# Attention scores of two heads on 64 array rows each, and an earlier fetch of cached keys and adaLN weights, in a two-layer hybrid decoder step

## The chip, the cores and the metric

The kernel runs on one core of a Trainium2 chip. The metric is the time of one execution on the device in microseconds (us), lower is better. Before the change three runs took 1097.65, 1100.09 and 1101.35 us; the median is 1100.09 us.

## The reference

One inference step of two decoder layers for a prompt of 512 tokens and eight sample rows that share all weights (width 1024, float32). Each layer is: adaLN-modulated RMSNorm, one input projection, two mixers, each times a SiLU gate, one output projection, adaLN gate, residual. Layer 0 has a short convolution and a windowed attention of 16 heads with 64 features; layer 1 has multi-scale pooling and retention. The change touches the attention of the prompt and the fetch of the cached keys for the sample rows. For the prompt it comes to this:

```python
q, k, v = (a.reshape(Bn, L, H_B, HD_B) for a in (q, k, v))      # 16 heads of 64
qf = q.astype(jnp.float32) * (Dh ** -0.5)
# scores q k^T plus ALiBi over three windows (128,1), (512,4), (2048,16),
# merged by their softmax denominators: one softmax with a bias that holds log(count)
y_b = o.reshape(Bn, L, W_B) * jax.nn.silu(gb)
```

The sample rows attend to 256 of 1024 cached keys and values in the same three patterns. k and v of all tokens are outputs too.

## The kernel before

Features lie on the partitions, tokens on the columns (512 of the prompt and 8 of the sample group). To reach float32 accuracy with the faster matmul type, each factor x is split into a high part (ACT copies x to the type fp32r) and a low part (VectorE, DVE, subtracts the high part from x); a product is then high × high, high × low and low × high.

A weight tile of 128 output features is computed by `product` (line 315): eight steps (k = 0 to 7), each with six matmuls of 256 or 264 columns (`mm3`, line 295). After each step `advance` (line 304) issues a part of the conversion of later weights: the high part on ACT at k = 1 (`w_hi`), low parts on DVE (`w_lo`), the load of a raw tile on SP (`w_raw`, four buffers). Then comes `tick` (line 198), the clock of the issue order. Small work is put into its queues: `at(n, ...)` runs n steps later; `put(..., after=n)` at the first step from n on, one per step; `put_fill` at a step in which no `put` was due; `put2` at even steps. The order of issue is thus written out by hand, and each engine, and SP's queue of DMA issues too, executes its instructions in that order.

Layer 0 begins with the attention, `head_pair(p)` (line 457), eight times. A pair has two heads (e = 0, 1) of 64 features, so that one weight tile is v, k, gate or q of both heads. The tiles come in the order v, k, gate, q, 32 steps in all; the scores and all that follows them run beside the tiles of the next pair. Times after the q tile are counted from its end, with Q0 = 5 as base for scores, turns and weighings.

- The plain k (`kf`, line 585) is copied by ACT out of PSUM. `k_dup` (line 473) then makes for each head a tile with that head's 64 rows of k twice, on partitions 0 to 63 and 64 to 127, with four DMAs from SBUF to SBUF. `k_split` (line 481), 7 and 9 steps after the k tile, makes high and low parts of each doubled tile.
- q (lines 600 to 612): for each head one tile with the high part of its 64 rows on its own half of the partitions and the low part on the other half (`q_lo`).
- `score(e, qb)` (line 508), four blocks of 128 queries for each head: two matmuls over all 128 rows, first with the high, then with the low part of the doubled k, with N = 256, 256, 384, 512 columns. DVE adds the bias and takes the minimum of the negated scores (line 521), ACT takes Exp one step later, `norm` (line 529) divides three steps later: DVE's reciprocal, then DVE (even blocks) or ACT (odd blocks) scales.
- `turn(e, g)` (line 539) transposes the probabilities on TensorE in three groups and splits them; `weigh(e, jb)` (line 547) multiplies them with v. Scores, turns, weighings, the turned v (`v_out`), the rows of q and the adaLN products share four PSUM buffers (`aux`).
- `q_rows` (line 487) turns q of the sample rows and writes it to DRAM. Four steps later `window_load` (line 495) loads it back, broadcast to all partitions, then the cached keys (three DMAs, 1 MB) and a tile of layer 1's adaLN weights (1 MB); both of these use the pool `big` with three buffers. DVE multiplies keys by q and sums (`window_scores`, `window_sums`, lines 568 and 572) 5 and 8 steps later; the adaLN product (`ada`, line 360) follows 8 steps later.

The order of the attention of one pair at the end of the q tile is written as:

```python
for e, fn, ticks in (
    (0, score, (0, 1, 3, 4)), (1, score, (6, 7, 9, 10)), (0, turn, (11, 13, 15)), (0, weigh, (18, 19, 21, 23)),
    (1, turn, (17, 20, 22)), (1, weigh, (25, 26, 27, 28)),
):
```

All DMAs go through SP's queue (`load`, line 156). After the attention come the convolution tiles of layer 0, the output projection and layer 1, which the change leaves alone.

Of the kernel before, what the change touches and what calls it, by code (L numbers as in the profile page):

```python
# [29 lines left out]

# columns of the packed constants
C_ID = 0
# [54 lines left out]
def hybrid_kernel(ctx: ExitStack, tc: tile.TileContext, a, o):  # L87
# [21 lines left out]
    def tr(n=T):  # L109
        return tt(n, F32R)  # L110
# [68 lines left out]

# [1 line left out]
    now, seqn = [0], [0]  # L181
# [34 lines left out]

# [1 line left out]
    csm = cp.tile([P, C_W], F32, name="csm")  # L218
# [21 lines left out]

# [1 line left out]
    w_in = [a["w_in_e"], a["w_in_o"]]  # L242
# [61 lines left out]
    def advance(k):  # L304
        # weights of the tiles that come next, a part at each step of this tile
        if k == 1 or (k == 5 and n_split[0] < cur[0] + 2):
            w_hi()
        if k in (3, 6):
            w_lo((0,))
        if k in (4, 7):  # L310
            w_lo((1,))
        if k in (5, 7) and n_raw[0] < n_split[0] + 4:
            w_raw()
# [15 lines left out]

# [1 line left out]
    def ada_load(layer, kind, j):  # L331
# [35 lines left out]

# [1 line left out]
    def h_hi(layer, j, xp, xs):  # L369
# [12 lines left out]

# [1 line left out]
    warm = cp.tile([P, 1], F32, name="warm")  # L384
# [62 lines left out]
    load(csm[:, P:C_W], a["c_small"][:, P:C_W])  # L447
# [1 line left out]
    yB, yA = [None] * KT, [None] * KT  # L449
# [7 lines left out]
    def head_pair(p):  # L457
# [14 lines left out]

        def k_dup(kf):
            st["kd"] = []
            for e in range(2):
                kd = tt(S)
                for h in range(2):
                    load(kd[64 * h:64 * h + 64], kf[64 * e:64 * e + 64])
                st["kd"].append(kd)

        def k_split(e):
            kh, kl = tr(S), tr(S)
            act(kh, st["kd"][e])
            at(2, lo_of, kl, st["kd"][e], kh)
            st["k", e] = (kh, kl)

        def q_rows():
            pq = aux([NB, P])
            nc.tensor.transpose(pq, zs[0][:, 32 + p, :], ident)
            qt = tt(P, p=NB)  # L490
            act(qt, pq)
            at(1, load, qdr[p], qt)
            at(4, window_load)

        def window_load():
            st["qb"] = t4().rearrange("p (b d) -> p b d", b=NB)
            load(st["qb"], qdr[p].partition_broadcast(P))
            kw = big().rearrange("p (t b d) -> p t b d", t=2, b=NB)
            c = a["cache_win_k"][0].rearrange("b s h d -> s b (h d)")[:, :, p * P:(p + 1) * P]
            load(kw[:, 0], c[896:1024])  # L500
            load(kw[0:96, 1], c[512:896].rearrange("(n s) b d -> n s b d", s=4)[:, 0])
            load(kw[96:128, 1], c[0:512].rearrange("(n s) b d -> n s b d", s=16)[:, 0])
            for t in range(2):
                at(5 + 3 * t, put2, window_scores, t, kw)
            raw = ada_load(1, "ss", p)
            at(8, ada, 1, "ss", p, raw)

        def score(e, qb):
            if qb == 0:
                st["bt"] = bt[e]  # L510
                st["mn", e], st["ls", e] = mk(cp, [P, 4], F32, "mn", 4), mk(cp, [P, 4], F32, "ls", 4)
                st["E", e] = []
            n, N = (qb + 1) * P, max(H0, (qb + 1) * P)
            kh, kl = st["k", e]
            mn, ls = st["mn", e][:, qb:qb + 1], st["ls", e][:, qb:qb + 1]
            s = aux([P, S])
            qs = st["q", e][:, qb * P:(qb + 1) * P]
            mm(s[:, 0:N], qs, kh[:, 0:N], True, False)
            mm(s[:, 0:N], qs, kl[:, 0:N], False, True)
            sb = tt(n)  # L520
            nc.vector.tensor_tensor_reduce(  # L521
                out=sb, in0=s[:, 0:n], in1=bt[e][:, S - n:S], scale=1.0, scalar=3e38, op0=ALU.add, op1=ALU.min,
                accum_out=mn,
            )
            st["E", e].append(sb)
            at(1, act, sb, sb, ACTF.Exp, mn, -1.0, ls)
            at(3, norm, e, qb)
# [49 lines left out]

        # v, k, q and gate tiles, each followed by what depends on it
        vps = ps01[0] if p == 0 else z_tile(0, 48 + p, h0)
# [7 lines left out]
        sample_z(0, 40 + p, kps)  # L587
        at(0, k_dup, kf)
        at(1, load, o["k_t"][p], kf)
        at(7, k_split, 0)  # L590
        at(9, k_split, 1)
        gps = z_tile(0, 56 + p, h0)
# [5 lines left out]
        for e in range(2):  # L598
            load(bt[e], a["c_bias"][2 * p + e])
        qps = z_tile(0, 32 + p, h0)  # L600
        for e in range(2):
            r = slice(64 * e, 64 * e + 64)
            st["q", e] = tr(S)
            act(p2(st["q", e][r]), qps[r, :, 0:H0], ACTF.Copy, scale=-0.125)

        def q_lo():
            for e in range(2):
                r, r_ = slice(64 * e, 64 * e + 64), slice(64 - 64 * e, 128 - 64 * e)
                stt(p2(st["q", e][r_]), qps[r, :, 0:H0], -0.125, p2(f(st["q", e][r])), ALU.mult, ALU.subtract)
            sample_z(0, 32 + p, qps)  # L610

        at(1, q_lo)
        for e, fn, ticks in (
            (0, score, (0, 1, 3, 4)), (1, score, (6, 7, 9, 10)), (0, turn, (11, 13, 15)), (0, weigh, (18, 19, 21, 23)),
            (1, turn, (17, 20, 22)), (1, weigh, (25, 26, 27, 28)),
        ):
            for i, n in enumerate(ticks):
                put(fn, e, i, after=Q0 + n)
        put_fill(q_rows, after=8)

# [6 lines left out]

# [1 line left out]
    uc = mk(cp, [P, KT, 15 + NB], F32, "uc", 1)[:, :, 0:2 + 2 * NB]  # L629
# [9 lines left out]
    def soft_scores():  # L639
        # softmax over window rows and the new row, (batch, head) on partitions  # L640
        prod = tt(P).rearrange("p (b k e) -> p b k e", b=NB, k=KT)
# [46 lines left out]
    def window_weigh(b0):  # L688
        # two batches at a time: rows (batch, half of the heads, head), columns (head in the half, feature)
        pd = aux([P, 512])  # L690
# [106 lines left out]

# [1 line left out]
    def out_tile(layer, m, ps, halves=(0, 1)):  # L799
# [15 lines left out]
    def scaled(j, out=None):  # L815
        # input of layer 1 without its norm's factor and without the shift
        x = xT[j] if out is None else out
        vtt(x[:, S:T], xT[j][:, S:T], mA[1][:, j, 0:NB], ALU.mult)
        act(x[:, 0:S], xT[j][:, 0:S], ACTF.Copy, scale=mA[1][:, j, 8:9])
        xT[j] = x  # L820
# [39 lines left out]

    # the first tiles of layer 1 take x without the norm's factor, which is put to their products
    h1, r1 = [[tr(), tr()] for _ in range(KT)], tt()
# [35 lines left out]

# [1 line left out]
    G = [1.0 - 2.0 ** (-5.0 - h) for h in range(H_D)]  # L900
# [6 lines left out]
    def ret_head(h):  # L907
# [97 lines left out]

        # sample group: state update and read, all batches of this head
        def v_rows():
# [64 lines left out]

        # tiles
        st["vh"] = t4(dt=F32R).rearrange("p (a i d) -> p a i d", a=4, i=2)
# [64 lines left out]

# [1 line left out]
    spl = t4()[:, 0:KT * NB * 15].rearrange("p (k b w) -> p k b w", k=KT, b=NB)  # L1141
# [76 lines left out]

# [1 line left out]
    xo = [[tt(512) for _ in range(2)] for _ in range(4)]  # L1220
# [14 lines left out]
    def rows(m, blocks):  # L1235
        # rows of tokens: their squares and their product with the gain
        hf, c = m // 4, (m % 4) * P
# [37 lines left out]

    # the last tile: one half of the tokens after the other
    m = KT - 1
# [25 lines left out]
def layout(i):  # L1303
    # the arrays in the order in which the tiles are read
    def tiles(w):
# [33 lines left out]
def results(r):  # L1339
    # features back to the last axis  # L1340
    conv = r["conv_t"].transpose(2, 1, 0).reshape(2 + 2 * NB, D)
# [29 lines left out]
```

## Time and profile before

| | us |
|---|---|
| median of three runs | 1100.09 |
| lowest, highest run | 1097.65, 1101.35 |
| profiled execution, first to last instruction (its span) | 1099.1 |
| TensorE matmuls (PE) busy | 1046.0 (95%) |
| VectorE (DVE) busy | 652.6 (59%) |
| ScalarE (ACT) busy | 501.5 (46%) |
| mean granted TensorE clock | 0.985 |

The profile is one execution on the chip; the page gives its span alone as its time, 1.0 us below the median of the runs. PE is the matmul part of TensorE and PEld its weight loads, which overlap with matmuls; SPq is SP's queue, which issues the DMAs. Busy time counts overlapping instructions once. An idle time is shown in square brackets with what ended it. The attention stage of the eight pairs lies at about 50 to 350 us. Engines work in parallel, so a busy engine need not be what sets the time.

### The profile page before, as it was taken

To read this page: it belongs to the slowest core of one execution; us is meant where nothing else is said; L and a number is where in the kernel's file an instruction comes from. 1 tells how busy PE (TensorE), PEld (TensorE's weight loads), DVE (VectorE), ACT (ScalarE), POOL (GpSimd) and SP (SyncE) were. 2 spreads that over 40 slices of the span, in tenths; PEclk is the share of its full clock that TensorE was granted. 3 is DMA by queue.
4 is the path that set the end of the run, shared out by engine and by line. 5 is a ranking of instruction groups with operands and counts; after the bars stand their busy time and mean duration, and the time that the engine had idled before them with its cause. 6 is when DMAs were issued, how large, how long until landed. Compare 5 with 4: busy or idle time off the path is not lost.

```text
span 1099.1 us, 21017 instructions
## 1 busy us (share of the span) xinstructions
PE 1046.0 (95%) x8592; PEld 1000.6 (91%) x8592; DVE 652.6 (59%) x1484; ACT 501.5 (46%) x906; POOL 27.4 (2%) x45
## 2 busy tenths in 40 slices
PE   3999899989989999999999989999999999999996
PEld 1698898889989899999999989999999999999996
DVE  6557676767668544446444487555746667664443
ACT  4575568556755322223243364545444444332333
POOL 3000000000000000000000040000000000000000
PEclk9899999999999999999999999999999999999998
DMA  8365654565446463542653326372543532225212
GB/s 350 149 218 182 201 179 147 166 213 184 140 158 192 154 205 125 192 157 83 205 204 130 120 69 235 112 249 87 206 164 117 195 124 87 87 87 184 97 68 78
DMA packets 84736, 173.15 MB, mean 158 GB/s; under 512 B 7720, under 2 KB 47752, under 8 KB 81560
## 3 DMA queue, kind: packets, MB, share of 16 engines
q1 hardware_dynamic: 84640, 171.81, 46.7%
q8 instruction: 67, 1.10, 0.4%
q14 instruction: 29, 0.24, 0.1%
HBM read 149.40 MB, written 18.65 MB: 153 GB/s over the span
## 4 chain that ended last, share of the span: by engine, by line
PE 77%; DMA 8%; DVE 6%; ACT 5%; issue 2%; SPq 1%; DVEq 0%; ACTq 0%
PE mm L160 64%; PE aux L160 11%; ACT t L140 4%; DMA t<-t 4%; DMA big<-in_cache_win_k 3%; DVE t L146 2%; DVE wlo L146 1%; SPq L157 1%; DVE t L521 1%; DMA wraw<-in_w_in_e 1%; DMA v<-vdr 1%; ACT whi L140 1%; DMA out_k_t<-t 1%; ACT L140 0%; PE aux L1242 0%
## 5 line engine op out<-in xcount | busy, mean ns | idle before, releaser
L160 PE MATMUL mm<-t,whi 128*128 128x256 f32 (+1 forms) x4608 | 766.0, 288 | 7.7 <-ACT t L140 5.6
L160 PEld LDWEIGHTS mm<-t,whi 128*128 128x128 f32 x4608 | 644.3, 190 | 31.6 <-issue 17.2
L160 PE MATMUL mm<-t,wlo 128*128 128x256 f32 (+2 forms) x2304 | 468.2, 284 | 0.0
L160 PEld LDWEIGHTS mm<-t,wlo 128*128 128x128 f32 x2304 | 361.2, 190 | 0.0
L146 DVE TENSOR_TENSOR wlo<-wraw,whi 128x512 fp32r<-128x512 f32 x288 | 194.3, 701 | 51.8 <-ACT whi L140 51.3
L140 ACT ACTIVATE whi<-wraw 128x1024 fp32r<-128x1024 f32 x144 | 151.8, 1054 | 96.9 <-PE mm L160 61.1
L140 ACT ACTIVATE t<-t 128x520 fp32r<-128x520 f32 (+3 forms) x124 | 75.8, 616 | 214.8 <-DVE t L149 98.3
L146 DVE TENSOR_TENSOR t<-t,t 128x520 fp32r<-128x520 f32 (+6 forms) x172 | 112.4, 654 | 96.4 <-ACT t L140 95.0
L140 ACT ACTIVATE t<-mm 128x512 f32<-128x512 f32 (+3 forms) x124 | 61.0, 512 | 126.6 <-PE mm L160 125.9
L140 ACT ACTIVATE t<-aux 128x512 fp32r<-128x512 f32 (+7 forms) x148 | 66.5, 465 | 57.7 <-PE aux L160 20.4
L146 DVE TENSOR_TENSOR t<-aux,t 128x512 fp32r<-128x512 f32 (+6 forms) x120 | 61.7, 514 | 24.0 <-ACT t L140 17.5
L160 PE MATMUL aux<-t,v 128*128 128x512 f32 (+2 forms) x224 | 52.3, 338 | 18.5 <-DVE t L146 18.5
L160 PE MATMUL aux<-t,t 128*128 128x256 f32 (+2 forms) x320 | 63.2, 311 | 0.0
L160 PEld LDWEIGHTS aux<-t,v 128*128 128x128 f32 x224 | 36.1, 197 | 21.5 <-DVE t L146 20.4
L143 DVE COPY zs<-mm 128x8 f32<-128x8 f32 x76 | 12.2, 161 | 60.6 <-ACT t L140 60.5
L160 PEld LDWEIGHTS aux<-t,t 128*128 128x128 f32 x320 | 47.0, 188 | 0.7
L140 ACT ACT_TABLE_LOAD x32 | 41.1, 1283 | 8.1 <-DVE mn L521 3.5
L140 ACT ACTIVATE t<-t,mn 128x128 f32<-128x128 f32 (+1 forms) x64 | 35.3, 551 | 12.9 <-DVE mn L521 12.8
L521 DVE CUSTOM_DVE_ANT_0 t<-aux,t 128x128 f32<-128x128 f32 (+1 forms) x64 | 30.7, 488 | 9.6 <-PE aux L160 9.4
L149 DVE SCALAR_TENSOR_TENSOR big<-v,ksc,big 128x256 f32<-128x256 f32 x64 | 27.7, 481 | 10.1 <-ACT big L140 9.7
L146 DVE TENSOR_TENSOR t<-mm,t 128x512 f32<-128x512 f32 (+1 forms) x24 | 16.6, 690 | 26.7 <-PE mm L160 17.4
L160 PE MATMUL aux<-big,scT 128*32 128x256 f32 x384 | 27.4, 406 | 0.3 <-DMA big<-in_ada_e 0.3
(145 smaller groups left out, 591.6 us busy)
## 6 DMA issues: line engine op xcount, KB each, us to landing
wraw<-in_w_in_e SPq DMA_DIRECT2D x64, 512.0 KB
wraw<-in_w_in_o SPq DMA_DIRECT2D x48, 512.0 KB
big<-in_ada_e SPq DMA_DIRECT2D x12, 1024.0 KB
big<-in_ada_o SPq DMA_DIRECT2D x12, 1024.0 KB
wraw<-in_w_out_e SPq DMA_DIRECT2D x16, 512.0 KB
big<-in_state_ret SPq DMA_DIRECT2D x16, 512.0 KB
out_new_ret_sample<-big SPq DMA_DIRECT2D x16, 512.0 KB
wraw<-in_w_out_o SPq DMA_DIRECT2D x16, 512.0 KB
```

What stands on the lines that cost most here:

```text
L140: return nc.scalar.activation(out=out, in_=in_, func=func, scale=scale, **kw)
L143: return nc.vector.tensor_copy(out, in_)
L146: return nc.vector.tensor_tensor(out=out, in0=in0, in1=in1, op=op)
L149: return nc.vector.scalar_tensor_tensor(out=out, in0=in0, scalar=scalar, in1=in1, op0=op0, op1=op1)
L157: return nc.sync.dma_start(out=out, in_=in_)
L160: nc.tensor.matmul(out, lhsT=lhsT, rhs=rhs, start=start, stop=stop)
L521: nc.vector.tensor_tensor_reduce(out=sb, in0=s[:, 0:n], in1=bt[e][:, S - n:S], scale=1.0, scalar=3e38, op0=ALU.add, op1=ALU.min, accum_out=mn,
```

## The change

- k is not copied any more: `k_dup` is gone, and `k_split` makes one high and one low tile of the plain k, 3 steps after the k tile. q too has one high and one low tile with both heads, each head on its own 64 partitions.
- A score call does both heads for one block of queries. It takes two PSUM buffers and issues three products (high × high, high × low, low × high), alternating between head 0 (partitions 0 to 63) and head 1 (64 to 127): six matmuls over 64 rows. What follows a score (`soft`) is as before, for one head and then the other.
- The scores run at steps 0, 2, 3, 5 after the base, the turns of both heads interleaved at 11 to 17, the weighings of head 0 at 18 to 21 and those of head 1 at 22 to 26.
- The cached keys and the adaLN weights are loaded by `window_load` 5 steps after the gate tile, that is in the q tile. The broadcast of q is a function of its own, `q_load`, four steps after `q_rows`, which may run from step 4 instead of 8. The key products come 7 and 10 steps after `q_load`, the adaLN product 20 steps after its load.

The rest of the diff removes comments. Its core:

```diff
-        def k_dup(kf):
-            st["kd"] = []
-            for e in range(2):
-                kd = tt(S)
-                for h in range(2):
-                    load(kd[64 * h:64 * h + 64], kf[64 * e:64 * e + 64])
-                st["kd"].append(kd)
-
-        def k_split(e):
+        def k_split(kf):
             kh, kl = tr(S), tr(S)
-            act(kh, st["kd"][e])
-            at(2, lo_of, kl, st["kd"][e], kh)
-            st["k", e] = (kh, kl)
+            act(kh, kf)
+            at(2, lo_of, kl, kf, kh)
+            st["k"] = (kh, kl)
...
-            at(4, window_load)
+            at(4, q_load)
 
         def window_load():
-            st["qb"] = t4().rearrange("p (b d) -> p b d", b=NB)
-            load(st["qb"], qdr[p].partition_broadcast(P))
             kw = big().rearrange("p (t b d) -> p t b d", t=2, b=NB)
...
+            st["kw"] = kw
+            raw = ada_load(1, "ss", p)
+            at(20, ada, 1, "ss", p, raw)
+
+        def q_load():
+            st["qb"] = t4().rearrange("p (b d) -> p b d", b=NB)
+            load(st["qb"], qdr[p].partition_broadcast(P))
             for t in range(2):
-                at(5 + 3 * t, put2, window_scores, t, kw)
-            raw = ada_load(1, "ss", p)
-            at(8, ada, 1, "ss", p, raw)
+                at(7 + 3 * t, put2, window_scores, t, st["kw"])
 
-        def score(e, qb):
+        def score(qb):
+            N = max(H0, (qb + 1) * P)
+            ss_ = [aux([P, S]) for _ in range(2)]
+            for c, (x, y) in enumerate(((0, 0), (0, 1), (1, 0))):
+                for e in range(2):
+                    r = slice(64 * e, 64 * e + 64)
+                    mm(ss_[e][:, 0:N], st["q"][x][r, qb * P:(qb + 1) * P], st["k"][y][r, 0:N], c == 0, c == 2)
+            for e in range(2):
+                soft(e, qb, ss_[e])
+
+        def soft(e, qb, s):
...
-            s = aux([P, S])
-            qs = st["q", e][:, qb * P:(qb + 1) * P]
-            mm(s[:, 0:N], qs, kh[:, 0:N], True, False)
-            mm(s[:, 0:N], qs, kl[:, 0:N], False, True)
...
-        at(0, k_dup, kf)
         at(1, load, o["k_t"][p], kf)
-        at(7, k_split, 0)
-        at(9, k_split, 1)
+        at(3, k_split, kf)
...
+        at(5, window_load)
         qps = z_tile(0, 32 + p, h0)
...
+        qh, ql = tr(S), tr(S)
+        st["q"] = (qh, ql)
+        act(p2(qh), qps[:, :, 0:H0], ACTF.Copy, scale=-0.125)
 
         def q_lo():
...
+            stt(p2(ql), qps[:, :, 0:H0], -0.125, p2(f(qh)), ALU.mult, ALU.subtract)
             sample_z(0, 32 + p, qps)
 
         at(1, q_lo)
+        for qb, n in enumerate((0, 2, 3, 5)):
+            put(score, qb, after=Q0 + n)
         for e, fn, ticks in (
-            (0, score, (0, 1, 3, 4)), (1, score, (6, 7, 9, 10)), (0, turn, (11, 13, 15)), (0, weigh, (18, 19, 21, 23)),
-            (1, turn, (17, 20, 22)), (1, weigh, (25, 26, 27, 28)),
+            (0, turn, (11, 13, 15)), (1, turn, (12, 14, 17)), (0, weigh, (18, 19, 20, 21)), (1, weigh, (22, 23, 24, 26)),
         ):
             for i, n in enumerate(ticks):
                 put(fn, e, i, after=Q0 + n)
-        put_fill(q_rows, after=8)
+        put_fill(q_rows, after=4)
```

## Rows read from the trace of the kernel before

**Rows 1.** The profile's page, busy time of the engines over the whole span.
```profile
PE 1046.0 (95%) x8592; PEld 1000.6 (91%) x8592; DVE 652.6 (59%) x1484; ACT 501.5 (46%) x906; POOL 27.4 (2%) x45
```

**Rows 2.** Windows, two head pairs: stretch, length, busy PE, PEld, DVE, ACT, POOL, PEclk, DMA, GB/s.
```profile
101.35:139.38 38.03, 34.48 (x272) 32.97 (x271) 25.32 (x62) 23.09 (x46) 0.00 (x0) 0.96 0.55 169
139.38:173.83 34.45, 32.82 (x272) 31.51 (x271) 25.32 (x62) 23.11 (x46) 0.00 (x0) 1.00 0.56 181
```

**Rows 3.** Waits of PE, 60 to 350 us: us in total, times, longest.
```profile
PE aux L160 <- DVE t L146: 18.5, 8, 3.5
```

**Rows 4.** Timeline of PE at three of these waits: start, us, instruction, idle before it.
```profile
96.72 0.50 PE L160 MATMUL aux<-t,v 128*128 128x512 f32 x1 [2.15 <-DVE t L146]
...
133.19 0.61 PE L160 MATMUL aux<-t,v 128*128 128x512 f32 x1 [3.55 <-DVE t L146]
...
204.47 0.50 PE L160 MATMUL aux<-t,v 128*128 128x512 f32 x1 [2.46 <-DVE t L146]
```

**Rows 5.** Windows, two equal stretches: behind the wait at 133.19, and later.
```profile
133.44:136.85 3.41, 3.41 (x15) 3.20 (x15) 2.69 (x5) 1.52 (x4) 0.00 (x0) 0.50 0.10 25
...
137.00:140.41 3.41, 3.41 (x31) 3.41 (x30) 1.80 (x4) 3.03 (x5) 0.00 (x0) 1.00 0.31 123
```

**Rows 6.** The chain of waits, 101 to 140 us: start, us, what.
```profile
120.65 8.38 DMA t<-t
...
129.11 0.63 ACT t L140
...
132.58 0.57 DVE t L146
```

**Rows 7.** Waits of ACT, 60 to 330 us.
```profile
ACT t L140 <- DMA t<-t: 47.7, 7, 8.0
...
ACT whi L140 <- DMA wraw<-in_w_in_e: 1.2, 1, 1.2
```

**Rows 8.** Timeline of SP's queue, 110 to 124 us: DMA issues.
```profile
112.73 4.21 SPq L157 DMA_DIRECT2D big<-in_cache_win_k  x3
116.99 1.69 SPq L157 DMA_DIRECT2D big<-in_ada_o  x1
...
119.29 3.46 SPq L157 DMA_DIRECT2D t<-t  x4
```

**Rows 9.** Windows, the stretch in which these transfers land; the last two columns are DMA.
```profile
118.50:130.50 12.00, 11.15 (x97) 10.03 (x95) 7.57 (x9) 2.98 (x6) 0.00 (x0) 1.00 1.03 310
```

**Rows 10.** Timeline of PE, 141 to 145.8 us: score matmuls (aux) and what follows each.
```profile
141.40 0.40 PE L160 MATMUL aux<-t,t 128*128 128x256 f32 x2
141.63 0.64 PE L160 MATMUL mm<-t,whi 128*128 128x256 f32 x4
...
145.08 0.63 PE L160 MATMUL aux<-t,t 128*128 128x512 f32 x2
145.55 0.52 PE L160 MATMUL mm<-t,whi 128*128 128x256 f32 x3
```

**Rows 11.** Timeline of PE, 126.6 to 129.6 us: an adaLN product between projection matmuls.
```profile
127.33 0.39 PE L160 MATMUL mm<-t,wlo 128*128 128x256 f32 x2
127.65 1.07 PE L160 MATMUL aux<-big,scT 128*32 128x256 f32 x16
128.65 0.75 PE L160 MATMUL mm<-t,whi 128*128 128x256 f32 x4
129.24 0.40 PE L160 MATMUL mm<-t,wlo 128*128 128x256 f32 x2
```

**Rows 12.** The page's groups, weight loads (all aux products of two tiles): busy, mean ns.
```profile
L160 PEld LDWEIGHTS aux<-t,t 128*128 128x128 f32 x320 | 47.0, 188 | 0.7
```

**Rows 13.** Windows, from a pair's first Exp to its last scaling.
```profile
105.58:118.64 13.06, 13.06 (x107) 12.87 (x107) 8.48 (x32) 11.69 (x29) 0.00 (x0) 1.00 0.50 151
```

**Rows 14.** Timeline of DVE, 121 to 129 us: key product and its sum.
```profile
122.03 1.23 DVE L146 TENSOR_TENSOR big<-big,v 128x1024 f32<-128x1024 f32 x1 [1.83 <-DMA big<-in_cache_win_k]
...
124.38 1.21 DVE L573 TENSOR_REDUCE t<-big 128x16 f32<-128x1024 f32 x1
```

More of the change, by code (lines that the diff above doesn't have):

```diff
@@ L502, in window_load @@
             load(kw[96:128, 1], c[0:512].rearrange("(n s) b d -> n s b d", s=16)[:, 0])
-            for t in range(2):
-                at(5 + 3 * t, put2, window_scores, t, kw)
-            raw = ada_load(1, "ss", p)
-            at(8, ada, 1, "ss", p, raw)
-        def score(e, qb):
+            st["kw"] = kw
[4 more added lines that the diff above has]
+            load(st["qb"], qdr[p].partition_broadcast(P))
+            for t in range(2):
+                at(7 + 3 * t, put2, window_scores, t, st["kw"])
[9 more added lines that the diff above has]
+        def soft(e, qb, s):
             if qb == 0:
-                st["bt"] = bt[e]
                 st["mn", e], st["ls", e] = mk(cp, [P, 4], F32, "mn", 4), mk(cp, [P, 4], F32, "ls", 4)
                 st["E", e] = []
-            n, N = (qb + 1) * P, max(H0, (qb + 1) * P)
-            kh, kl = st["k", e]
+            n = (qb + 1) * P
             mn, ls = st["mn", e][:, qb:qb + 1], st["ls", e][:, qb:qb + 1]
-            s = aux([P, S])
-            qs = st["q", e][:, qb * P:(qb + 1) * P]
-            mm(s[:, 0:N], qs, kh[:, 0:N], True, False)
-            mm(s[:, 0:N], qs, kl[:, 0:N], False, True)
             sb = tt(n)
@@ L599, in head_pair @@
             load(bt[e], a["c_bias"][2 * p + e])
+        at(5, window_load)
         qps = z_tile(0, 32 + p, h0)
[L601 to L604, printed above, removed]
+        qh, ql = tr(S), tr(S)
+        st["q"] = (qh, ql)
+        act(p2(qh), qps[:, :, 0:H0], ACTF.Copy, scale=-0.125)
         def q_lo():
-            for e in range(2):
-                r, r_ = slice(64 * e, 64 * e + 64), slice(64 - 64 * e, 128 - 64 * e)
-                stt(p2(st["q", e][r_]), qps[r, :, 0:H0], -0.125, p2(f(st["q", e][r])), ALU.mult, ALU.subtract)
+            stt(p2(ql), qps[:, :, 0:H0], -0.125, p2(f(qh)), ALU.mult, ALU.subtract)
             sample_z(0, 32 + p, qps)
         at(1, q_lo)
+        for qb, n in enumerate((0, 2, 3, 5)):
+            put(score, qb, after=Q0 + n)
         for e, fn, ticks in (
-            (0, score, (0, 1, 3, 4)), (1, score, (6, 7, 9, 10)), (0, turn, (11, 13, 15)), (0, weigh, (18, 19, 21, 23)),
-            (1, turn, (17, 20, 22)), (1, weigh, (25, 26, 27, 28)),
+            (0, turn, (11, 13, 15)), (1, turn, (12, 14, 17)), (0, weigh, (18, 19, 20, 21)), (1, weigh, (22, 23, 24, 26)),
         ):
```

## The prediction

> **What bounds the kernel now.** First the busy shares: TensorE (PE) is busy for 1046.0 of 1099.1 us [rows 1], so work of another engine counts only where PE waits for it. The windows show the period of a head pair in the attention stage: pairs have the same 272 matmuls and the same work on ScalarE (ACT) and VectorE (DVE), yet one lasts 38.03 us and the next 34.45 us [rows 2]; so some of a pair is waiting. The waits of PE name it: between 60 and 350 us PE waits 8 times, once for each pair, always on DVE, 18.5 us together [rows 3]. Three of the eight stand in [rows 4], 2.15, 3.55 and 2.46 us long, in front of the first matmul of head 1's weighted sum.
>
> A wait can cost twice. Behind the 3.55 us of idleness the granted clock is 0.50, that is 1.2 GHz instead of 2.4: 15 matmuls in 3.41 us, where an equal stretch at 1.00 holds 31 [rows 5]. Four of the eight waits (2.46 us and longer) are followed by such a stretch, the four of 2.15 us and shorter by none [rows 4].
>
> The chain of waits tells why: ACT stands for some 8 us before the first copy of the doubled k, which waits for the DMA from SBUF to SBUF. Head 1's turned probabilities queue behind it on ACT, then on DVE (the 384-column low part at 132.58), which frees the PSUM buffer for PE's weighted sum [rows 6]. ACT loses 47.7 us in seven such waits [rows 7]. Why the DMA is late, SP's queue tells: the cached keys take SP 4.21 us to issue, the adaLN weights 1.69 us, and only then come the four copies, 3.46 us [rows 8]. Between 118.5 and 130.5 us the 16 DMA engines are full (share 1.03, 310 GB/s) [rows 9]: the copies travel among 2 MB that nobody needs yet.
>
> **The change part by part.**
> *The copy of k goes.* With it go four DMAs and 3.46 us of SP [rows 8] and the DMA wait of ACT [rows 7] in each pair. k is split in place: one ACT copy of 0.63 us instead of two [rows 6] and one DVE subtraction less; q loses one of two on each engine too. All that lies beside PE's work, so I count no gain for it alone. What counts is the eight waits, −18.5 us, and the four half-clock stretches, each losing half of 3.41 us, −6.8 us.
>
> Late next would be DVE. The two key products and their two sums (1.2 us each [rows 14], 4.9 together) now fall among the low parts. PE's first weighing, at step 18, takes one of the four auxiliary PSUM buffers, which the low part of head 1's second group must have left. From the first turn (step 11) to there PE has 7 steps of 0.72 us (six matmuls at 0.12 [rows 10]), six turns of 0.44 and the adaLN block of 1.0 [rows 11]: 8.7 us. DVE has 4.9 of keys and four low parts (0.57 with 384 columns [rows 6], a third more with 512): 2.7, and starts half a microsecond late: 8.1 us. It just fits; I add 0.3 us a pair, +2.4 us.
>
> *Scores.* Now a call is two matmuls of full 128 rows for one head; two of 256 columns take 0.24 us and two of 512 take 0.47 us from start to next start [rows 10]; 384 lies between (0.35). A pair costs 2 × (0.24 + 0.24 + 0.35 + 0.47) = 2.6 us. After, a call is three products for both heads on 64 rows each: three rounds, if the two heads run side by side. No 64-row matmul is in the trace. The nearest row is the adaLN product, whose matmuls use 32 columns of the array: 16 take 1.00 us [rows 11], 0.06 us each where one on the whole array with as many columns takes 0.12, so parts of the array do run together. But entering and leaving costs: 127.33 to 127.65 where two matmuls need 0.24 us (+0.08), 128.65 to 129.24 where four need 0.47 us (+0.12), and inside the 1.00 us up to 0.1 more. I take 0.28 us a call. Then the calls cost 0.28 + 3 × (0.12, 0.12, 0.175, 0.235) = 0.64, 0.64, 0.81, 0.99: 3.1 us a pair, 0.5 more than now, +3.8 us for eight pairs. Bounds: side by side without surcharge, 1.95 us (−5 us in all); one head after the other with it, 5.0 us (+19 us). I take the middle value since both of its parts are seen in rows 11.
>
> A matmul here comes every 0.12 us [rows 10] although its weight load lasts 0.19 us [rows 12], so loads run under matmuls on the same rows. The Trainium skill says otherwise: in "TensorE: Matmul & The Clock Gate", Part 3 (Packing small matmuls — row/col tiling), a weight load overlaps with running matmuls only where its row group differs. By that rule the rounds of a head would show their loads, and the time would be that of the third rival; on the full array this trace does not agree with it.
>
> *Softmax of both heads at once.* Scores now run at steps 0, 2, 3, 5 for both heads, and the turns at 11 to 17. At present ACT is busy for 11.69 of the 13.06 us from the first Exp to the last scaling [rows 13]. Some 2.3 us of that (a turned part, the plain k, one weight part, the small q copy) falls outside the new stretch, and head 1's last scaling (0.7) comes after head 0's: 8.7 us until head 0 is ready. PE has 11 steps of 0.72 us, 3.1 us of scores and 0.4 us of v's turn, 11.4 us, less 1.1 us until the first Exp can start: 10.3 us. ACT also waited 1.4 us in that stretch (13.06 − 11.69). So head 0's last probabilities come about when PE turns them; with DVE's weight parts in front of the last reciprocal I put them 0.4 us late, +3.2 us for eight pairs. Bounds: nothing, and 2.4 us a pair, just under what halved the clock.
>
> *Fetches.* Keys and adaLN weights are issued at step 5 of the q tile, 17 steps earlier. The adaLN fetch needs the big buffer of the keys before, whose sums now end at step 19 of their pair, ten steps ahead. Behind both on SP stand raw weights of later tiles: a single weight conversion of ACT waited for one in this stage, 1.2 us [rows 7]. The broadcast of q has 8 steps until its use, no longer with the 2 MB; at present DVE waited 1.83 us before a key product [rows 14]. The adaLN product comes 20 steps after its fetch instead of 8, with the same work. I take nothing for these; a late broadcast would hold up the low parts (second rival).
>
> Sum against the profiled execution's 1099.1 us: −18.5 − 6.8 + 2.4 + 3.8 + 3.2 = −15.9, so 1083.2. The median of the three runs is 1100.09, 1.0 higher, so 1084 us.
>
> **The rivals.**
> First, the two heads' score matmuls do not overlap. For it: none of 64 rows is in the trace, and both write all 128 PSUM partitions. Against: rows 11. Price: +19.4 instead of +3.8, while the longer scores give the softmax its 3.2 us back: 1097. Chance 0.13.
> Second, the low parts stay late behind the key products on DVE (broadcast late, or DVE too full). For it: the balance of 8.1 against 8.7 us. Price: 1.5 us a pair instead of 0.3, without loss of clock, +10: 1094. Chance 0.10.
> Third, weight loads exposed in the second and third round of a call: 2 × 0.19 us × 4 calls × 8 = 12 us: 1096. Chance 0.03, as rows 10 and 12 speak against it.
> Fourth, on the other side: the softmax of two heads at once makes a new long wait in front of head 0's turn. It decides at about 2.4 us a pair, because from there the clock halves and 1.7 us is added [rows 5]: 4.1 us against the 2.4 us a pair ((18.5 + 6.8 − 2.4 − 3.8) / 8) that is to be gained. For it: ACT is 90% busy in the stretch [rows 13]. Against: the balance above. With 3.5 us: 8 × 5.2 = 42 us, so 1084 − 3 + 42 = 1123. Chance 0.12.
>
> **How the numbers follow.** My own case has 0.62: 1084, from 1075 (no late turn, no late low part, a third of the surcharge) to 1091 (a turn late by 1.3 us). The first three rivals lie at 1094 to 1097. The range 1075 to 1097 leaves out the fourth and half of the first. A measurement of this kernel can tell about 0.3% (3.3 us) from no change, so faster is under 1096.8: my case, the second, the third, half of the first: 0.81. Same 0.07; slower 0.12.
>
> **What would show it.** Right: no wait of ACT on a copy, no PE wait before head 1's first weighing, granted clock 1.00 throughout the stage, pairs of about 33.7 us; score matmuls of 64 rows in twos, starting a few ns apart, and some 0.1 us more before and behind each call. Short PE waits in front of the first turn or head 0's first weighing, under 1 us, are my two late terms. Wrong: 64-row matmuls at 0.12 us one behind the other (first rival), waits of over a microsecond before weighings with DVE at the key products (second), gaps of a weight load between rounds (third), waits of over 2.4 us before turns with clock 0.50 behind them (fourth).

## The result and the profile after

The changed kernel takes 1080.47 us (median of four runs, 1080.08 to 1080.71) against 1098.97 us before on the same chip: a ratio of 0.983 (95% interval 0.982 to 0.985). The prediction was 1084, range 1075 to 1097.

The page of the changed kernel, span and busy shares, answers to [rows 1]:

```profile
span 1078.3 us, 21052 instructions
...
PE 1042.2 (97%) x8656; PEld 989.0 (92%) x8656; DVE 638.1 (59%) x1468; ACT 492.3 (46%) x890; POOL 27.4 (3%) x45
```

Two head pairs of the changed kernel in windows (columns as in [rows 2]):

```profile
112.89:146.27 33.38, 33.38 (x280) 31.00 (x279) 23.45 (x60) 21.98 (x43) 0.00 (x0) 1.00 0.57 173
146.27:179.75 33.48, 33.48 (x281) 31.09 (x279) 23.46 (x60) 21.96 (x43) 0.00 (x0) 1.00 0.57 174
```

The waits of PE in the changed kernel, 60 to 350 us [rows 3]:

```profile
PE aux L160 <- DVE t L146: 2.0, 3, 0.9
```

The pairs no longer differ: PE is busy in all of each, the clock is 1.00, and the eight waits of 18.5 us have become three short ones: two in the last pair (0.89 us at 319.26 us, 0.63 us at 323.06 us) and one behind it (0.49 us at 339.74 us). The waits of ACT, 60 to 330 us, answer to [rows 7]; the DMA of the copy is gone from them, and the raw weights are no later than before:

```profile
ACT t L140 <- PE aux L160: 37.8, 15, 4.5
ACT t L140 <- PE aux L543: 14.5, 25, 0.9
...
ACT whi L140 <- DMA wraw<-in_w_in_e: 0.6, 1, 0.6
```

ACT now waits for PE, which is how it should be in a stage that PE bounds. The timeline of SP's queue, 146 to 180 us [rows 8], has the two megabytes in the q tile and the broadcast of q by itself:

```profile
155.95 4.83 SPq L157 DMA_DIRECT2D big<-in_cache_win_k  x3
160.88 0.40 SPq L157 DMA_DIRECT2D big<-in_ada_o  x1
...
169.57 0.33 SPq L157 DMA_DIRECT2D v<-qdr  x1
```

A score call in the timeline of PE [rows 10]: two projection matmuls, the call, four projection matmuls, two more.

```profile
133.87 0.39 PE L160 MATMUL mm<-t,wlo 128*128 128x256 f32 x2
134.19 0.63 PE L160 MATMUL aux<-t,t 64*128 64x256 f32 x6
134.75 0.75 PE L160 MATMUL mm<-t,whi 128*128 128x256 f32 x4
135.33 0.41 PE L160 MATMUL mm<-t,wlo 128*128 128x256 f32 x2
```

The form 64*128 says that each uses 64 rows of the array. Six matmuls of 256 columns take 0.56 us from first start to the next projection matmul, so the two heads do run side by side: six in a row at 0.12 us each would need 0.72. Before them 0.32 us pass where two matmuls need 0.24, behind them 0.58 where four need 0.47. From the matmul before a call to the second one behind it, less what the projection needs there, the calls cost (medians over the stage) 0.75 us with 256 columns, 0.92 with 384 and 1.09 with 512, where a pair of 128-row matmuls cost 0.24, 0.35 and 0.47. A head pair's scores are 2 × 0.75 + 0.92 + 1.09 = 3.5 us instead of 2 × (2 × 0.24 + 0.35 + 0.47) = 2.6: 7.2 us more for eight pairs.

### The profile page after: what moved, and what is told of

Its sections match the earlier page's. It is cut to its first block, busy times and chain, and to the rows that moved or that the text cites. A ratio compares the mean times of both kernels' runs of the same rounds, so it can differ in the third digit from the quotient of the medians.

```text
span 1078.3 us, 21052 instructions
## 1 busy us (share of the span) xinstructions
PE 1042.2 (97%) x8656; PEld 989.0 (92%) x8656; DVE 638.1 (59%) x1468; ACT 492.3 (46%) x890; POOL 27.4 (3%) x45
## 4 chain that ended last, share of the span: by engine, by line
PE 92%; DVE 4%; ACT 2%; DMA 1%; issue 1%; SPq 0%; DVEq 0%; ACTq 0%
PE mm L160 75%; PE aux L160 13%; PE aux L543 2%; DVE t L146 1%; ACT t L140 1%; DVE wlo L146 1%; DMA v<-vdr 1%; PE aux L348 0%; PE aux L1239 0%; DVE t L149 0%; DMA t<-in_x_t 0%; PE aux L463 0%; DVE t L202 0%; PE aux L918 0%; ACT whi L140 0%
## 5 line engine op out<-in xcount | busy, mean ns | idle before, releaser
L160 PEld LDWEIGHTS mm<-t,whi 128*128 128x128 f32 x4608 | 637.3, 189 | 36.2 <-issue 21.9
L146 DVE TENSOR_TENSOR t<-t,t 128x520 fp32r<-128x520 f32 (+6 forms) x164 | 107.0, 652 | 96.3 <-ACT t L140 94.6
L140 ACT ACTIVATE t<-t 128x520 fp32r<-128x520 f32 (+3 forms) x116 | 70.9, 616 | 166.0 <-DVE t L149 97.8
L140 ACT ACTIVATE t<-aux 128x128 f32<-128x128 f32 (+7 forms) x148 | 67.9, 469 | 115.9 <-PE aux L160 64.8
L140 ACT ACTIVATE t<-mm 128x512 f32<-128x512 f32 (+2 forms) x116 | 56.4, 507 | 114.0 <-PE mm L160 112.5
L160 PE MATMUL aux<-t,t 64*128 64x256 f32 (+6 forms) x384 | 56.2, 329 | 0.0
L521 DVE CUSTOM_DVE_ANT_0 t<-aux,t 128x128 f32<-128x128 f32 (+3 forms) x64 | 28.9, 489 | 31.9 <-PE aux L160 31.4
L160 PEld LDWEIGHTS aux<-t,t 64*128 64x128 f32 (+1 forms) x384 | 41.5, 186 | 5.4
L140 ACT ACTIVATE t<-t,mn 128x128 f32<-128x128 f32 (+3 forms) x64 | 35.4, 554 | 13.3 <-DVE mn L521 13.1
L350 DVE TENSOR_REDUCE m<-aux 128x18 f32<-128x72 f32 x24 | 5.5, 231 | 45.8 <-PE aux L348 45.8
```

What stands on the lines that cost most here:

```text
L140: return nc.scalar.activation(out=out, in_=in_, func=func, scale=scale, **kw)
L146: return nc.vector.tensor_tensor(out=out, in0=in0, in1=in1, op=op)
L160: nc.tensor.matmul(out, lhsT=lhsT, rhs=rhs, start=start, stop=stop)
L350: nc.vector.tensor_reduce(out=m, in_=pt.rearrange("p s (g r) -> p s r g", g=4)[:, :, 0:9, :], op=ALU.add, axis=AX.X)
L521: nc.vector.tensor_tensor_reduce(out=sb, in0=s[:, 0:n], in1=bt[e][:, S - n:S], scale=1.0, scalar=3e38, op0=ALU.add, op1=ALU.min, accum_out=mn,
```

## The experiments

Each run was compared with the kernel before on its own chip. Theory: what cost time was the copy of k arriving late, and it was late because of what stood in front of it in SP's queue; the new form of the scores costs time. Rivals are in the expectations.

**The fetch alone.** The kernel before, with `window_load` in the q tile and `q_load` split off as in the change, and nothing else:

```diff
-            at(4, window_load)
+            at(4, q_load)
...
+        at(5, window_load)
         qps = z_tile(0, 32 + p, h0)
```

> The kernel before, with only the fetch of keys and adaLN weights moved into the q tile; the doubled k still comes by four DMAs and the scores are 128-row products. My theory (the copies are late only because 2 MB stand in front of them): ACT's waits on the copy fall from 47.7 us to under 10, PE's eight waits from 18.5 us to under 5, no half clock, and since the scores keep their cheap form (2.6 us a pair instead of 3.5) the time is 1073 to 1077 us, below the changed kernel. Rival (the copy is slow by itself: four issues of SP and their landing): ACT still waits several microseconds a pair, PE over 10 us in all, 1085 to 1095 us.

Measured: 1071.26 us, ratio 0.974 (0.971 to 0.977). Less than the changed kernel, whose interval lies wholly above. A pair of this run in windows:

```profile
144.03:176.57 32.54, 32.54 (x272) 31.44 (x270) 25.07 (x61) 23.12 (x46) 0.00 (x0) 1.00 0.65 197
```

Its waits of PE, 60 to 350 us:

```profile
PE aux L160 <- DVE t L146: 0.5, 1, 0.5
```

The timeline of its SP queue in the same pair:

```profile
145.72 2.40 SPq L157 DMA_DIRECT2D t<-t  x4
...
152.16 4.50 SPq L157 DMA_DIRECT2D big<-in_cache_win_k  x3
156.76 1.73 SPq L157 DMA_DIRECT2D big<-in_ada_o  x1
```

The four copies stand ahead of the two megabytes now, and ACT's waits no longer list them at all, though they are as many and as large as ever. The pair takes 32.5 us, 0.9 less than in the changed kernel: that is the difference of the scores. So the theory holds in both halves, and the rival (the copy is slow by itself) falls.

**One megabyte at a time.** The kernel before with the keys alone moved:

```diff
+            st["kw"] = kw
...
+                at(5 + 3 * t, put2, window_scores, t, st["kw"])
+            raw = ada_load(1, "ss", p)
+            at(8, ada, 1, "ss", p, raw)
```

> The kernel before with the cached keys alone moved into the q tile; the adaLN weights are still fetched right before the four copies of k. My theory (the copies are late by what stands in front of them, SP's issues and 2 MB): 1 MB and 4.2 us of SP less brings them some 6 us forward, so ACT's waits on the copy fall below 20 us, PE's waits below 5 us and no clock is lost: 1071 to 1077 us. Rival (each megabyte counts alike towards PE's wait): half of the gain, about 1085 us.

Measured: 1072.18 us, ratio 0.976 (0.974 to 0.979). And with the adaLN weights alone moved:

```diff
+        def ada_early():
+            raw = ada_load(1, "ss", p)
+            at(20, ada, 1, "ss", p, raw)
...
+        at(5, ada_early)
         qps = z_tile(0, 32 + p, h0)
```

> The kernel before with the adaLN weights alone moved into the q tile; broadcast of q and keys are still issued right before the four copies of k. My theory: 1 MB and 1.7 us of SP less bring the copies 3 to 5 us forward, ACT waits 10 to 25 us for them in all; PE's waits, at most 3.5 us now, fall to a few microseconds without clock loss: 1073 to 1080 us. Rival (the keys, 4.2 us of SP, are what delays the copies): PE's waits stay over 10 us and 1088 us or more.

Measured: 1073.41 us, ratio 0.977 (0.974 to 0.980). The line on the copy in ACT's waits (60 to 330 us), first of the run with early keys:

```profile
ACT t L140 <- DMA t<-t: 7.7, 7, 2.7
```

and of the run with early weights:

```profile
ACT t L140 <- DMA t<-t: 11.5, 7, 2.7
```

Either megabyte out of the way takes ACT's 47.7 us to 8 or 12, under 3 us at a time, and PE then waits no longer than in the run with both moved (0.5 us in all, behind the last pair); the pairs last 32.5 us in all three runs. The cost was not in proportion to the bytes: a wait of ACT counts only from the point where PE's work ahead of it runs out, and half of the cure reaches that point. Both rivals fall: half of the fetch does not bring half of the gain, and the keys alone are not what delays the copies.

**The copy gone, fetch late.** The changed kernel with the fetch at its old place:

```diff
-        at(5, window_load)
...
-            at(20, ada, 1, "ss", p, raw)
+            at(8, ada, 1, "ss", p, raw)
...
+            window_load()
             for t in range(2):
-                at(7 + 3 * t, put2, window_scores, t, st["kw"])
+                at(5 + 3 * t, put2, window_scores, t, st["kw"])
...
-        put_fill(q_rows, after=4)
+        put_fill(q_rows, after=8)
```

> The changed kernel with the fetch put back to its old time (behind the broadcast of q, 14 steps into the next pair); no copy of k, scores on 64 rows. My theory (the copy was all that anything waited for): PE's waits stay under 5 us in the attention stage, 1079 to 1085 us; DVE waits for keys up to 2 us a pair beside other work. Rival (the early fetch is needed too, since late keys hold up the low parts on DVE): PE waits 8 us or more before weighings or turns, 1088 us or more.

Measured: 1147.83 us, ratio 1.043 (1.039 to 1.047), and neither case as I had put it. The waits of PE, 60 to 350 us:

```profile
PE aux L160 <- DMA big<-in_ada_o: 33.4, 5, 7.5
PE aux L160 <- DVE wlo L146: 14.0, 2, 7.1
```

PE stands about 7 us a pair in front of the adaLN product (the two waits of the second row are in front of it too). In the order of the kernel before, the steps from 8 after the fetch on were taken by turns and weighings, so the product ran 15 steps after it, by luck of the list; in the new one a step is free just there. The run therefore says little of the keys. The same with the product 17 steps after its fetch:

```diff
-            at(8, ada, 1, "ss", p, raw)
+            at(17, ada, 1, "ss", p, raw)
```

> The run with the copy gone and the fetch at its old time, but with the adaLN product 17 steps after its fetch instead of 8 (in the earlier run PE stood in front of that product for the weights, about 7 us a pair). My theory (the early fetch matters to the changed order only through the adaLN product, which finds a free step there 8 steps after its fetch; late keys hold up DVE, which has room): PE waits under 6 us in the stage, 1080 to 1087 us. Rival (late keys hold up the low parts as well): PE waits 1.5 us or more a pair before turns or weighings, 1092 us or more.

Measured: 1108.41 us, ratio 1.009 (1.006 to 1.012): my theory fell, the rival holds. The waits of DVE in this run, 60 to 350 us:

```profile
DVE big L146 <- DMA big<-in_cache_win_k: 34.1, 7, 5.3
```

Its waits of PE in the same stretch:

```profile
PE aux L160 <- DVE t L146: 21.3, 14, 2.5
```

The timeline of DVE at one of these waits:

```profile
200.99 1.23 DVE L146 TENSOR_TENSOR big<-big,v 128x1024 f32<-128x1024 f32 x1 [4.98 <-DMA big<-in_cache_win_k]
202.13 0.55 DVE L146 TENSOR_TENSOR t<-aux,t 128x384 fp32r<-128x384 f32 x1
```

And that of PE behind it:

```profile
202.74 0.50 PE L160 MATMUL aux<-t,v 128*128 128x512 f32 x1 [2.23 <-DVE t L146]
```

DVE stands 5 us before the first key product, the low parts stand behind it, and PE waits for the PSUM buffer that a low part frees, twice a pair. So without the early fetch, the removal of the copy with the new order of turns is no gain at all: the wait has only changed its DMA, and the scores cost 7.2 us more. Whether the removal would gain with a late fetch and the old order of the turns was not tried.

**The copy on the engines.** The early fetch, 128-row scores, and the doubled k written by ACT and DVE across the two halves of the partitions:

```diff
+            act(kh[r], kf[r])
+            act(kh[r_], kf[r])
+            at(2, k_low, e, kf, kh, kl)
...
+            lo_of(kl[r], kf[r], kh[r])
+            lo_of(kl[r_], kf[r], kh[r])
```

> The kernel before with the fetch moved as in the change, and the doubled k written by ACT (four copies of 64 rows a pair) and DVE (four subtractions) instead of by DMA; scores are 128-row products as before. My theory (a pair is bound by PE once nothing waits for a DMA): no half clock, PE waits under 3 us in the stage, scores at 2.6 us a pair: 1072 to 1076 us, below the changed kernel by the 7 us that its scores cost more. Rival (ACT and DVE, with some 2 us a pair more work each than in the changed kernel, become late): PE waits of a microsecond or more a pair before turns or weighings, 1082 us or more.

Measured: 1072.91 us, ratio 0.975 (0.972 to 0.978). A pair in windows:

```profile
144.94:177.65 32.71, 32.71 (x273) 31.47 (x271) 26.77 (x63) 24.68 (x48) 0.00 (x0) 1.00 0.57 175
```

ACT and DVE carry 2.7 and 3.3 us a pair more than in the changed kernel and nothing becomes late (PE's only wait from 60 to 350 us is one of 0.5 us). It confirms that the pair is bound by PE; it does not beat the run with the fetch alone.

**What a score call pays.** The six matmuls in another order, head 0's three and then head 1's three:

```diff
-            for c, (x, y) in enumerate(((0, 0), (0, 1), (1, 0))):
-                for e in range(2):
+            for e in range(2):
+                for c, (x, y) in enumerate(((0, 0), (0, 1), (1, 0))):
```

> The changed kernel with the six matmuls of a score call in another order: the three of head 0, then the three of head 1. My theory (two heads run at the same time only when their matmuls are neighbours): only head 0's last and head 1's first overlap, five rounds instead of three, two more of 0.12, 0.12, 0.17, 0.23 us: 1.3 us a pair, +10 us, 1090 to 1092 us. Rival (no order matters, the engine finds the pairs itself): 1080 to 1082 us. Rival (no overlap at all in this order): +15 us, 1095 to 1097 us.

Measured: 1082.68 us, ratio 0.984 (0.980 to 0.987). That is 0.7 us above the range of the first rival and 2.2 us (0.2%) above the changed kernel, less than the runs of the kernel before differ among themselves; the spans of the two profiled executions agree (1078.5 and 1078.3). The call in PE's timeline takes 0.56 us as before:

```profile
133.95 0.63 PE L160 MATMUL aux<-t,t 64*128 64x256 f32 x6
134.51 0.75 PE L160 MATMUL mm<-t,whi 128*128 128x256 f32 x4
```

The trace has their starts in twos, 10 ns apart (133.947 and 133.957, 134.172 and 134.181, 134.294 and 134.302), though the program lists three of one head first. In this call the fifth and the sixth matmul signal a semaphore and the third does not, though head 0's last stands third in the list: the twos are one matmul of either head. That the list's order reached the engine is not written in the trace, but the first two of a call start 10 ns apart in all calls here and 3 or 4 ns apart in all calls of the changed kernel. My theory of neighbours falls: the engine starts matmuls of the other 64 rows ahead of their turn.

Calls joined in twos:

```diff
-        for qb, n in enumerate((0, 2, 3, 5)):
-            put(score, qb, after=Q0 + n)
+        for qbs, n in (((0, 1), 0), ((2, 3), 4)):
+            put(score, qbs, after=Q0 + n)
```

> The changed kernel with score calls joined in twos (blocks 0 and 1, then 2 and 3): twelve 64-row matmuls in a row instead of six. My theory (a call pays some 0.39 us for entering and leaving the 64-row form, whatever it holds): four entries fewer in a pair are halved to two, 2 x 0.39 us x 8 = -6 us, 1074 to 1076 us, if the four PSUM buffers are free in time. Rival (each 64-row matmul is slower by itself): no change, 1079 to 1081 us. Rival (all four buffers at once make PE wait): 1081 us or more, with PE waits before scores.

Measured: 1076.27 us, ratio 0.980 (0.977 to 0.982). Twelve matmuls in PE's timeline:

```profile
134.09 0.98 PE L160 MATMUL aux<-t,t 64*128 64x256 f32 x12
135.00 0.76 PE L160 MATMUL mm<-t,whi 128*128 128x256 f32 x4
```

Measured as above, the joined calls cost 1.10 us (256 columns twice) and 1.61 (384 and 512), where two single ones cost 2 × 0.75 and 0.92 + 1.09: 0.40 us less in both, whatever they hold. The pairs are 0.8 us shorter (32.7 against 33.4), 6 us for eight. The span fell by 3.6 us only (1074.7 against 1078.3), since the start, before the stage, took 1.4 us longer in this profiled execution and some of the rest came back behind it; my number was reached in the stage and missed in the time by a little.

Each head in a call of its own, with nothing to run beside it:

```diff
+        def score(e, qb):
...
+            for c, (x, y) in enumerate(((0, 0), (0, 1), (1, 0))):
+                mm(s[:, 0:N], st["q"][x][r, qb * P:(qb + 1) * P], st["k"][y][r, 0:N], c == 0, c == 2)
```

> The changed kernel with each head's score call by itself again, at the steps of the kernel before: three matmuls of 64 rows with no second head to run beside them. My theory (a 64-row matmul lasts as long as one of 128 rows, 0.12 us for 256 columns; side by side it costs nothing more; each entry into the 64-row form and out of it costs 0.40 us): a pair's scores take 8 x 0.40 + 2 x 1.95 = 7.1 us instead of 3.5, +28 us, 1105 to 1111 us, no waits added. Rival (half the rows, half the time): 8 x 0.40 + 1.95 = 5.2 us, +13 us, about 1094 us. Rival (the 0.40 us comes from two heads writing at once, not from entering): 3.9 us and little more, about 1084 us.

Measured: 1107.98 us, ratio 1.008 (1.006 to 1.011), as forecast, and no wait of PE in the stage but one of 0.54 us in the last pair (at 350.22 us). Three matmuls without a partner:

```profile
142.02 0.63 PE L160 MATMUL aux<-t,t 64*128 64x256 f32 x3
142.58 0.75 PE L160 MATMUL mm<-t,whi 128*128 128x256 f32 x4
```

0.56 us again, as long as six with a partner. So the second head is free, half the rows save nothing, and the surcharge is paid for each entry.

## Why the prediction was right, and where its terms were off

*The waits and the clock* (−18.5 and −6.8): right in place and cause, and near in size. PE's waits are down to 2.0 us, the half-clock stretches are gone from the stage, and the chain that the prediction read (keys and weights on SP, then the copies, then ACT, then DVE, then PE) was taken apart by three runs that leave the copy in and only clear its way. A wait costs a little more than its idle time says: 0.17 us from start to start at the 1.63 us wait at 169.18 us of before (start to start 1.92, less one matmul of 0.12, is 1.80). The fetch alone, which ends these waits and leaves the scores as they were, took 28.9 us off (1100.16 to 1071.26) where the two terms have 25.3. Eight times 0.17 us is 1.4 of the 3.6 between them; most of the rest lies before and behind the stage in the two profiled executions, where nothing was changed.

*Scores* (+3.8): the mechanism was right, the size was not. They cost +7.2 us. The step that failed is "I take 0.28 us a call", read off the adaLN product, where the inside of the block could only be bounded. It is 0.40: 0.09 us before the first matmul, 0.10 in the first round (its start to the second's is 0.22 instead of 0.12), 0.09 after the last round and 0.10 at the first full-row matmul behind. The Trainium skill, "TensorEngine Tiling (Array Packing)", Key Properties, says that a change of tiling mode drains TensorE; all three forms of call agree with it, at 0.40 us for there and back.

*Softmax of both heads* (+3.2) and *low parts behind the keys* (+2.4): neither came in the first seven pairs. The balance for ACT was right, the lateness put on top of it was not. From the first Exp to the last scaling ACT is busy for 9.36 us (forecast: 8.7 for head 0 and 0.7 for head 1), in windows:

```profile
168.67:179.69 11.02, 11.02 (x90) 9.82 (x89) 7.84 (x31) 9.36 (x24) 0.00 (x0) 1.00 0.40 128
```

and the timeline of ACT at the first turn, with head 0's scaling, shows how close it was:

```profile
178.35 1.34 ACT L140 ACTIVATE t<-t,ls 128x512 f32<-128x512 f32 x2
```

The timeline of PE at the same place:

```profile
179.16 0.40 PE L160 MATMUL mm<-t,wlo 128*128 128x256 f32 x2
179.39 0.60 PE L543 MATMUL aux<-csm,t 128*128 128x128 f32 x4
```

Head 0's scaling, the first of the two, ends at 179.08 (0.72 us each), the turn starts at 179.39 without a wait. A longer score call (0.40 instead of 0.28) gave ACT 0.5 us more as well. The second rival's mechanism is real: the run with late keys shows it, and so, in small, does the last pair of the changed kernel. The timeline of DVE there:

```profile
318.53 0.68 DVE L146 TENSOR_TENSOR t<-aux,t 128x512 fp32r<-128x512 f32 x1
319.13 1.22 DVE L146 TENSOR_TENSOR big<-big,v 128x1024 f32<-128x1024 f32 x1
320.26 0.55 DVE L146 TENSOR_TENSOR t<-aux,t 128x384 fp32r<-128x384 f32 x1
320.73 1.21 DVE L573 TENSOR_REDUCE t<-big 128x16 f32<-128x1024 f32 x1
321.85 0.68 DVE L146 TENSOR_TENSOR wlo<-wraw,whi 128x512 fp32r<-128x512 f32 x1
322.45 0.55 DVE L146 TENSOR_TENSOR t<-aux,t 128x384 fp32r<-128x384 f32 x1
```

and that of PE:

```profile
319.26 1.07 PE L160 MATMUL aux<-big,scT 128*32 128x256 f32 x16 [0.89 <-DVE t L146]
...
323.06 0.73 PE L160 MATMUL aux<-t,v 128*128 128x512 f32 x2 [0.63 <-DVE t L146]
```

The low part that ends at 323.00 stands behind a key product, its sum and a weight part, and PE waits for it before head 0's first weighing: the sign that the prediction named for its late terms. The one that ends at 319.21 stands behind the first key sum and the first work of a convolution tile (315.68 to 318.61), which only the last pair has beside it; with the fetch alone the first key product comes after that work (at 313.80 us, the work ends at 311.02), and PE does not wait there. The two waits are 1.5 us, once, where the term had 0.3 us in each pair.

That 1084 came so near to 1080.5 is in part luck: the scores cost 3.4 us more than forecast, the two late terms 5.6 us less but for the last pair, and the waits were worth 3.6 us more. The first and third rival fall with the timeline of a call, the fourth with the windows.

The limit by which the fourth rival was priced (half clock from a wait of about 2.4 us on) is what the kernel before shows, and it does not hold beyond it. In the run with late keys and the later adaLN product, the timeline of PE has these two waits:

```profile
128.53 0.50 PE L160 MATMUL aux<-t,v 128*128 128x512 f32 x1 [2.02 <-DVE t L146]
...
240.57 0.50 PE L160 MATMUL aux<-t,v 128*128 128x512 f32 x1 [2.49 <-DVE t L146]
```

and these are the windows behind them (columns as in [rows 2]):

```profile
129.75:133.16 3.41, 3.12 (x15) 2.82 (x14) 3.41 (x6) 1.54 (x2) 0.00 (x0) 0.50 0.77 287
...
240.57:248.00 7.43, 6.07 (x43) 5.69 (x43) 7.43 (x12) 2.14 (x3) 0.00 (x0) 1.00 0.79 293
```

A wait of 2.02 us is followed by the half clock, one of 2.49 us is not. The length of the one wait alone does not decide.

What the prediction missed is the other half of the question: it priced the parts against the kernel before, together, and never the fetch without the rest. Its own numbers held the answer: −25.3 for waits that any cure of the late copy ends, +3.8 for scores that only one cure needs. The fetch alone is 9 us faster than the whole change: 7 us are the scores, and about 2 us the stretch of the last pair, the four convolution tiles behind its q tile, in windows of the changed kernel and of the fetch alone:

```profile
297.54:332.42 34.88, 33.36 (x275) 30.70 (x274) 25.98 (x67) 18.13 (x38) 0.51 (x4) 1.00 0.38 131
...
291.44:323.46 32.02, 32.02 (x267) 30.93 (x266) 27.40 (x69) 19.96 (x40) 0.34 (x3) 1.00 0.38 119
```

Of the 2.9 us between them, 0.9 are the scores and 1.5 the two short waits above. No run took these waits away, so their cause is read from the trace alone.

## What to carry to other kernels

A transfer that is late in an in-order queue is often cured by moving what stands in front of it and is not needed soon; ask that before removing the transfer, and price each part of a change by itself. Once the worst waits fall under the slack of the engine that bounds the stage, clearing more brings nothing. Packing short contractions on parts of the array has to earn back 0.40 us for each entry: here a full-row form with two products (2.6 us a pair) beat three packed products in calls of six (3.5) and was level with calls of twelve (2.7).

## What was not expected of the hardware

Matmuls on different 64-row halves of the array start together even where the program lists three of one half first (0.56 us for six in either order; 10 ns apart in that order and 3 or 4 ns in the other, for the first two of a call). The Trainium skill, "TensorE: Matmul & The Clock Gate", Part 3, says that matmuls start and end in program order; the run with heads in turn does not agree. And entering and leaving the 64-row form costs 0.40 us whether 3, 6 or 12 matmuls are inside.
